# Stick-breaking attention with side work between its steps: other estimates for where the side work goes

## The chip, the cores and the metric

The kernel runs on one core of a Trainium2 chip. The metric is the device time of one execution in microseconds (us); less is better. Engines: TensorE (PE) for matmuls, VectorE (DVE), ScalarE (ACT), GpSimd (POOL), and SyncE (SP), which issues most DMA transfers.

## The reference, cut to what matters

One layer of a decoder trunk, 1024 positions of width 1024, in FP32. The part that the change touches is the mixer:

```
h = rms_norm(x, norm_mix_pre)
q, k, v, cb, cc, cx, g_att, g_conv = split(h @ w_in)
z = q.k / 8                              # 8 heads x 64, strictly causal
w[t,s] = sigmoid(z[t,s]) * prod_{s<j<t} (1 - sigmoid(z[t,j]))
y_att  = (w @ v) @ w_att_branch
y_conv = (cb * causal_dwconv3(cc * cx)) @ w_conv_branch
x = x + rms_norm((sigmoid(g_att)*y_att + sigmoid(g_conv)*y_conv) @ w_out, norm_mix_post)
```

A feed-forward block with a convolution follows (1024 to 2 x 2816, gelu, 2816 to 1024).

## The kernel before, in words

Every FP32 operand is split into a high and a low FP16 half, and a product is three matmuls (`PASSES`). So each weight tile of 512 KB needs work of its own before use: a load, a sum of squares (ACT, `square`), its total over partitions by a tiny matmul with ones (`total`), a power-of-two scale (three small DVE instructions, L89 to L92), the high half (ACT, L605) and the low half (DVE, L608).

**The attention loop.** There are 48 units, one for each pair of heads `j` (0 to 3), half of the queries `c`, and block `i` of 128 keys, taken from the last visible block down. `width` is the part of 512 queries that a unit touches (0.25 to 1). A turn `k` of the loop issues, in this order: `sums` of unit k (matmuls into the PSUM tile A, which exists once), `scores` of unit k+2 (matmuls into z, which exists once), a first stretch of fill, then `carry` and `sp_high` of k+1, `expa` of k, `sp_low` of k+1, `expz` of k+2, `times` of k, `bound` of k+2, `w_high_` of k, a second stretch of fill, then `softplus` of k+2, `w_low_` of k, `weigh` of k-1 (matmuls into o), and a third stretch of fill. The order on PE, DVE and ACT is exactly the one written (`manual_schedule`); each engine runs its own queue in order.

Two chains of waits cross the turns. `sums` of k+1 needs `carry`, `sp_high` and `sp_low` of k+1, and these need A of turn k; and `scores` of k+2 needs `expz` of k+1 to have read z.

**The fill.** Between those steps PE works on 400 chunks of three matmuls of 512 columns: the rest of v, the q, k, cb, cc, cx projections, the two gate projections (in the order of `FILL`), and last the tiles 4 to 7 of the convolution branch (`branch_fill`, output rows named ywc). Eight chunks fill one PSUM bank, and three banks are there for it (`bank`). A plan made before the loop says how many chunks each turn gets: `est[k]` is the estimated length of turn k, `att_pe[k]` the attention's own PE time in it, `lam` the factor that makes the total come out at 400 chunks of 0.65 us, and n = (est[k] * lam - att_pe[k]) / 0.65. The first stretch runs to 0.35 n, the second to 0.65 n, the third to n (`run_to`).

**The side work.** What the fill needs of ACT and DVE (evictions of banks, weight conversions, taps of the convolution, conversions of its result p to FP16 halves, L711 and L715) waits in lists of tasks in the class `Side`. At three points of each turn `point` adds `free[k]` to a credit of ACT and one of DVE, no higher than `CAP`, and lets tasks go ahead in order, evictions' list first. A step is issued while its engine's credit is above 0, or above a lower threshold where the task holds a bank or is urgent (`soon`); its cost is then taken off. What has not been done when a bank, a weight or (at branch tile 4, `q.drain`) the converted p is needed is forced: issued on the spot, whatever the credit. A weight's `total` borrows the bank of an eviction just done, and that bank is free only when the scale has been computed from it.

After the loop the gates go through a sigmoid, and the rest of the mixer and the feed-forward block follow; there the order of instructions is laid out by a scheduler and not written by hand.

Of the kernel before, what the change touches and what calls it, by code (L numbers as in the profile page):

```python
# [20 lines left out]
AF = mybir.ActivationFunctionType  # L21
ALU = mybir.AluOpType
# [6 lines left out]
NH = 512  # L29
# [1 line left out]
NFF = FF // P  # L31
EPS = 1e-6
EMAX = 1.2e19
FILL = ("q0 k0 q1 k1 cc0 cx0 q2 k2 cb0 cc1 cx1 cb1 cc2 cx2 q3 k3 cb2 cc3 cx3 cb3 gc0 ga0").split()
GROUPS = (2, 4, 4, 4, 4, 4)
KH = KD // 2
PASSES = ((0, 0), (0, 1), (1, 0))
# [2 lines left out]
class Layer:  # L40
# [235 lines left out]
    def mixer(self, mid):  # L276
        tc, nc, a = self.tc, self.nc, self.a
        hT = self.hp.tile([P, 2, KD, T], F16, tag="hT", name="hT")
        with ExitStack() as ph1:
# [368 lines left out]
            cv, dep, tail, last = {}, {}, [], [None]  # L648
# [92 lines left out]
            def branch(bi, d, pm, later=None):  # L741

                which = ("wc", "wa")[bi]
                w, inv = self.wdone[f"{which}{d // 2}"] if later else self.prep(f"{which}{d // 2}")
                outs = []
                sc = sgn[:, 4 * bi + d // 2:4 * bi + d // 2 + 1]
                if d % 2 == 0:
                    self.mul(sc, inv_x[bi], inv)
                y = self.xp.tile([P, T], F32, tag="x", name=f"y{which}{d}") if (bi, d) in ((0, 0), (0, 1)) else \
                    self.slot([P, T], F32, f"y{which}{d}")  # L750
                for c in range(2):
                    ps = bank(f"py{which}{d}_{c}") if later else pm.tile([P, NH], F32, tag="pm", name=f"py{which}{d}_{c}")
                    n = 0
                    for k in range(4):
                        for wi, hi in PASSES:
                            nc.tensor.matmul(ps, w[0][:, wi, ds((d % 2) * NH + k * P, P)],  # L756
                                             acts[bi][k][:, hi, ds(c * NH, NH)], start=n == 0, stop=n == 11)
                            n += 1
                        yield
                    if later:  # L760
                        def out(ps=ps, c=c):
                            last[0] = nc.vector.tensor_scalar(y[:, ds(c * NH, NH)], ps, sc, None, ALU.mult)
                        outs.append(Op("V", 0.7, out, f"py{which}{d}_{c}"))
                        later(outs[c:])
                    elif pm is self.pz:
                        nc.scalar.activation(y[:, ds(c * NH, NH)], ps, AF.Copy, scale=sc)
                    else:
                        nc.vector.tensor_scalar(y[:, ds(c * NH, NH)], ps, sc, None, ALU.mult)
                if later:
                    tail.append(lambda: self.sumsq(y, smy[:, 8 * bi + d:8 * bi + d + 1], f"y{which}{d}"))  # L770
                else:
                    self.sumsq(y, smy[:, 8 * bi + d:8 * bi + d + 1], f"y{which}{d}")
                ys[which, d] = y
# [3 lines left out]
            nu = len(units)  # L777
# [99 lines left out]
            def width(k):  # L877
                return (NH - units[k]["off"]) / NH if 0 <= k < nu else 0.0
# [19 lines left out]

            total, chunk = 400, 0.65
            att_pe = [2.6 * (width(k) * 0.33 + width(k + 2) * 0.33 + width(k - 1) * 0.33) for k in range(nu + 1)]  # L900
            est = [2.6 + 1.05 * (2 * width(k) + width(k + 1) + 2 * width(k + 2)) for k in range(nu + 1)]
            est[nu - 1] += 2.0
            est[nu] += 4.0
            att_v = [2.4 * (width(k) + width(k + 1) + 0.3 * width(k + 2)) * 0.9 for k in range(nu + 1)]
            lam = (sum(att_pe) + (total - 18) * chunk) / sum(est)
            free = [(est[k] * lam - att_v[k]) / 3 + 0.3 * (k > 36) for k in range(nu + 1)]
            fill = fills()
            state = dict(now=0.0)

            def run_to(t):  # L910
                while q.done < total and q.done < t:
                    if next(fill, "end") == "end":
                        q.done = total
                        return
                    q.done += 1
                    pump()

            with tc.manual_schedule(engines={ET.PE, ET.DVE, ET.Activation}):
                pump()
                run_to(6)  # L920
                at(scores, 0)
                at(expz, 0)
                at(bound, 0)
                q.point()
                run_to(10)
                at(softplus, 0)
                q.point()
                at(scores, 1)
                at(sp_high, 0)
                at(sp_low, 0)  # L930
                at(expz, 1)
                at(bound, 1)
                run_to(14)
                q.point()
                at(softplus, 1)
                run_to(18)
                q.point()
                base = 18.0
                for k in range(nu + 1):
                    n = (est[k] * lam - att_pe[k]) / chunk  # L940
                    at(sums, k)
                    at(scores, k + 2)
                    run_to(base + 0.35 * n)
                    at(carry, k + 1)
                    at(sp_high, k + 1)
                    at(expa, k)
                    if ready:
                        ready.pop(0)[1]()
                    q.point(free[k])
                    at(sp_low, k + 1)  # L950
                    at(expz, k + 2)
                    at(times, k)
                    at(bound, k + 2)
                    at(w_high_, k)
                    q.point(free[k])
                    run_to(base + 0.65 * n)
                    at(softplus, k + 2)
                    at(w_low_, k)
                    at(weigh, k - 1)
                    q.point(free[k])  # L960
                    run_to(base + n)
                    if ready:
                        ready[0][0]()
                    base += n
                run_to(total)
                for _ in fill:
                    pass
                for f in ready.pop(0) if ready else ():
                    f()
                q.drain("end")  # L970
                for name, t in wtasks.items():
                    if any(o.eng == "sum" for o in t.ops):
                        for o in t.ops[:2]:
                            if o.cost == 1.2:
                                o.f()
                        st = next(o.st for o in t.ops if o.st)
                        self.wraw[name] = st["sm"], [st["t"]]
                    else:
                        q.force(t, name)
                for which in ("gc", "ga"):  # L980
                    nc.scalar.activation(sig[which, 0], sig[which, 0], AF.Sigmoid)
# [423 lines left out]
class Side:  # L1405


    CAP = 1.3

    def __init__(self, pm, ones, nc):  # L1410
        self.pm, self.ones, self.nc = pm, ones, nc
# [47 lines left out]
    def advance(self, t, force=False):  # L1459
        while t.ops:  # L1460
            op = t.ops[0]
            if op.eng == "sum":
                if force:
                    host = getattr(t, "host", None)
                    if host is None:
                        if t in self.waiting:
                            self.waiting.remove(t)
                        ps = self.tile(f"pr_{len(self.late)}")
                        self.total(ps, op.st["rb"])
                        t.ops.pop(0).f(ps)  # L1470
                    while host and t.ops and t.ops[0] is op:
                        self.step(host)
                    continue
                if t not in self.waiting and not hasattr(t, "host"):
                    self.waiting.insert(0 if op.cost < 0 else len(self.waiting), t)
                return
            if not force:
                if t.t >= self.clock or not all(o.done for o in op.needs):
                    return
                if op.eng and self.credit[op.eng] <= (-1.5 if any(o.soon for o in t.ops) else 0):  # L1480
                    return
            if op.eng:
                self.credit[op.eng] -= op.cost
            self.step(t)
            if not op.eng or not t.ops or t.ops[0].eng != op.eng:
                t.t = self.clock
# [23 lines left out]
class Pair:  # L1510
# [3 lines left out]
    A = {1: (0, 0), 2: (0, 1), 3: (3, 0), 4: (1, 1), 5: (2, 0), 6: (2, 1), 7: (1, 0)}  # L1514
# [55 lines left out]
class Gates(Pair):  # L1570


    def out(self, name):
        return self.l.xp.tile([P, T], F32, tag="x", name=name)
# [93 lines left out]
```

## Time and profile before

| | us |
|---|---|
| median of 3 runs (lowest to highest) | 1352.25 (1351.61 to 1354.85) |
| the profiled execution | 1350.92 |
| its span, first to last instruction | 1349.2 |
| PE busy | 1311.9 |
| DVE busy | 1050.8 |
| ACT busy | 859.1 |

The mean granted TensorE clock of the profiled execution was 0.998 of full speed. The attention loop lies between about 69 and 425 us of the span: its 192 matmuls into A are 48 turns of four, the first at 69.0 us. Busy times are unions of the instructions' times on an engine. In rows of a group, the figures after the bar are the busy time in us, the mean length of one instruction in ns, then the engine's idle time just before them and what ended it. In rows of waits they are the total in us, the number and the longest.

### The profile page before, as it was taken

The numbers are of one execution on the slowest core, as the hardware profiler recorded it, in microseconds if no ns is written. First come the engines' busy times: TensorE is split into PE (matmuls) and PEld (weight loads), VectorE is DVE, ScalarE is ACT, GpSimd is POOL, SyncE is SP. The second block draws the span as 40 slices with busy tenths as digits, with TensorE's granted clock in tenths as the row PEclk, the third lists the DMA queues.
The fourth block names the chain that finished last, engine by engine and source line by source line (L and its number), as shares of the span: only waits on it lengthen the run. The fifth ranks groups of instructions, "written<-read, shape, count | busy, mean of one in ns | idle before, by whom it ended". The sixth has DMA issues, their size and how long they took to land. (4 is left out here: it accounts for less than half of the span.)

```text
span 1349.2 us, 16783 instructions
## 1 busy us (share of the span) xinstructions
PE 1311.9 (97%) x6491; PEld 590.0 (44%) x6491; DVE 1050.8 (78%) x1697; ACT 859.1 (64%) x1205; POOL 34.5 (3%) x58
## 2 busy tenths in 40 slices
PE   5999999999998999999999999999999999999997
PEld 3544444344433444444444444444444444444443
DVE  6568887878878957878788977975894896699855
ACT  6578877877777966665555676743752762576524
POOL 2000000000000000000110000000000000000002
PEclk9999999999999999999999999999999999999999
DMA  7011201101001222241431123222220312313126
GB/s 267 33 33 32 63 32 32 36 28 48 32 16 32 63 63 66 76 177 57 137 114 44 51 63 126 63 63 94 63 94 1 125 63 63 125 34 123 63 48 109
DMA packets 26608, 96.12 MB, mean 71 GB/s; under 512 B 3088, under 2 KB 3216, under 8 KB 26528
## 3 DMA queue, kind: packets, MB, share of 16 engines
q1 hardware_dynamic: 25088, 89.80, 20.2%
q0 software_dynamic: 1440, 5.24, 2.1%
q8 instruction: 51, 0.84, 0.3%
q14 instruction: 29, 0.24, 0.1%
HBM read 86.61 MB, written 8.42 MB: 70 GB/s over the span
## 5 line engine op out<-in xcount | busy, mean ns | idle before, releaser
L1538 PEld LDWEIGHTS <-wh_u 128*128 128x128 f16 x1848 | 178.8, 98 | 217.6 <-issue 3.8
L1312 PE MATMUL pd<-wdh,f 128*128 128x512 f16 (+1 forms) x1068 | 230.2, 377 | 2.7 <-ACT wdh L97 1.1
L1312 PEld LDWEIGHTS <-f 128*128 128x128 f16 x1068 | 104.5, 98 | 126.9 <-issue 4.0
L97 ACT ACTIVATE wh_u<-ws_u,sc 128x1024 f16<-128x1024 f32 (+1 forms) x66 | 64.7, 999 | 103.6 <-DVE sc L80 80.0
L1319 DVE SCALAR_TENSOR_TENSOR yacc<-pd,sd,yacc 128x512 f32<-128x512 f32 (+1 forms) x81 | 58.6, 742 | 73.4 <-PE pd L1312 65.9
L1538 PEld LDWEIGHTS <-wh_g 128*128 128x128 f16 x588 | 56.9, 98 | 68.7 <-issue 0.4
L1123 PE MATMUL py<-wh_wo,m 128*128 128x512 f16 x384 | 83.9, 379 | 0.0
L98 DVE SCALAR_TENSOR_TENSOR wh_u<-ws_u,sc,wh_u 128x1024 f16<-128x1024 f32 (+1 forms) x66 | 72.4, 1103 | 9.5 <-ACT wh_u L97 9.4
L824 ACT ACTIVATE sh<-sp 128x1024 f16<-128x1024 f32 (+3 forms) x48 | 40.4, 841 | 53.4 <-DVE sp L819 53.1
L1615 DVE SCALAR_TENSOR_TENSOR ugu<-cgu,cw_g,ugu 128x1023 f32<-128x1023 f32 (+1 forms) x44 | 56.4, 1283 | 11.3 <-ACT ugu L1613 10.9
L828 DVE TENSOR_TENSOR sh<-sp,sh 128x1024 f16<-128x1024 f32 (+3 forms) x48 | 45.9, 956 | 18.0 <-ACT sh L824 17.8
L1615 DVE SCALAR_TENSOR_TENSOR ua<-cau,cw_a,ua 128x1023 f32<-128x1023 f32 (+1 forms) x44 | 56.3, 1280 | 1.4 <-ACT ua L1613 1.3
L1123 PEld LDWEIGHTS <-m 128*128 128x128 f16 x384 | 37.5, 98 | 44.1
L819 DVE TENSOR_TENSOR sp<-A,sp 1x1024 f32<-1x1024 f32 (+3 forms) x40 | 35.9, 897 | 25.4 <-PE A L781 21.7
L850 ACT ACTIVATE w<-e 128x1024 f16<-128x1024 f32 (+3 forms) x48 | 40.5, 843 | 21.3 <-DVE e L845 20.4
L854 DVE SCALAR_TENSOR_TENSOR w<-e,w 128x1024 f16<-128x1024 f32 (+3 forms) x48 | 45.8, 954 | 9.2 <-ACT w L850 9.2
L814 ACT ACTIVATE sp<-e,one 128x1024 f32<-128x1024 f32 (+3 forms) x48 | 44.4, 925 | 6.0 <-DVE e L809 3.1
L845 DVE TENSOR_TENSOR e<-e,g 128x1024 f32<-128x1024 f32 (+3 forms) x48 | 45.7, 953 | 1.9 <-ACT g L841 1.8
L58 ACT ACTIVATE jk_u<-ws_u 128x1024 bf16<-128x1024 f32 x44 | 46.4, 1054 | 0.8
L756 PE MATMUL pywc<-p,wh_wc 128*128 128x512 f16 x192 | 43.2, 379 | 3.5 <-ACT sga L730 1.1
L211 PE MATMUL pcb<-hT,wh_cb 128*128 128x512 f16 x192 | 44.9, 379 | 0.9 <-DVE sc_cb L89 0.8
L800 ACT ACTIVATE e<-z,cz 128x1024 f32<-128x1024 f32 (+3 forms) x48 | 43.0, 897 | 3.6 <-PE z L781 3.6
(697 smaller groups left out, 2623.3 us busy)
## 6 DMA issues: line engine op xcount, KB each, us to landing
ws_u<-w_up_nt SPq DMA_DIRECT2D x44, 512.0 KB
ds<-w_down SPq DMA_DIRECT2D x22, 512.0 KB
wd<-w_down SPq DMA_DIRECT2D x22, 512.0 KB
ws_g<-w_in_nt SPq DMA_DIRECT2D x14, 512.0 KB
x<-x SPq DMA_DIRECT2D x8, 512.0 KB
ws_wo<-w_out SPq DMA_DIRECT2D x8, 512.0 KB
xr<-x SPq DMA_DIRECT2D x8, 512.0 KB
out<-x SPq DMA_DIRECT2D x7, 512.0 KB
```

Of the source, the lines that this page charges most:

```text
L58: self.nc.scalar.activation(self.junk(f"jk_{name}"), src, AF.Square, accum_out=acc)
L97: self.nc.scalar.activation(dst[:, 0, :], src, AF.Copy, scale=s)
L98: self.nc.vector.scalar_tensor_tensor(dst[:, 1, :], src, s, dst[:, 0, :], ALU.mult, ALU.subtract)
L211: nc.tensor.matmul(ps, w[:, wi, ds(k * P, P)], hT[:, hi, k, ds(c * NH, NH)], start=n == 0, stop=n == last)
L828: nc.vector.tensor_tensor(sh[:, 1, :, off:], u["sp"][:, :, off:], sh[:, 0, :, off:], ALU.subtract)
L845: nc.vector.tensor_tensor(e[:, :, off:], e[:, :, off:], u["g"][:, :, off:], ALU.mult)
L854: nc.vector.scalar_tensor_tensor(w[:, 1, :, off:], u["e"][:, :, off:], 2.0 ** 14, w[:, 0, :, off:], ALU.mult, ALU.subtract)
L1123: nc.tensor.matmul(ps, m16[k][:, hi, ds(tt * P, P)], wo[k][:, wi, sl], start=k == 0 and p == 0, stop=k == 7 and p == 2)
L1312: nc.tensor.matmul(pd[nh], f16[g][k][:, hi, ds(tt * P, P)], w[k][:, wi, ds(*part)], start=run is runs[0] and n == 0, stop=run is runs[-1] ...
L1319: nc.vector.scalar_tensor_tensor(y[:, sl], ps, sm[:, 0:1], y[:, sl], ALU.mult, ALU.add)
L1538: nc.tensor.matmul(ps, w[wt][:, wi, ds(wc * NH + k * P, P)], self.block(i, hi, k), start=first and n == 0, stop=n == 3 * KH - 1, skip_grou ...
L1615: nc.vector.scalar_tensor_tensor(u[:, lag:], c[:, :T - lag], sm[:, 2 - lag:3 - lag], u[:, lag:], ALU.mult, ALU.add)
```

## The change

- The estimate of a turn weighs `width(k)` and `width(k + 2)` by 1.9 instead of 2; 0.5 is added for turn 43 (`nu - 5`, with nu = 48), 2 for turn 44, 1 for turn 46 and 1 for turn 22. What was added for turns 47 and 48 stays.
- The estimate of DVE's own time in a turn is multiplied by 0.95 instead of 0.9, and `free` gets 0.4 instead of 0.3 added after turn 36.
- The second stretch of fill ends at 0.6 n instead of 0.65 n.
- The credit is held at 0.8 instead of 1.3, and an urgent step is issued while the credit is above -0.5 instead of -1.5.
- The two gate projections change places in the fill and in the order of weight loads.
- The two evictions of convolution branch tile 5 go to ACT (a copy with a scale) instead of DVE.

```diff
--- before.py
+++ after.py
@@ -31,7 +31,7 @@
 NFF = FF // P
 EPS = 1e-6
 EMAX = 1.2e19
-FILL = ("q0 k0 q1 k1 cc0 cx0 q2 k2 cb0 cc1 cx1 cb1 cc2 cx2 q3 k3 cb2 cc3 cx3 cb3 gc0 ga0").split()
+FILL = ("q0 k0 q1 k1 cc0 cx0 q2 k2 cb0 cc1 cx1 cb1 cc2 cx2 q3 k3 cb2 cc3 cx3 cb3 ga0 gc0").split()
 GROUPS = (2, 4, 4, 4, 4, 4)
 KH = KD // 2
 PASSES = ((0, 0), (0, 1), (1, 0))
@@ -758,9 +758,12 @@
                             n += 1
                         yield
                     if later:
-                        def out(ps=ps, c=c):
-                            last[0] = nc.vector.tensor_scalar(y[:, ds(c * NH, NH)], ps, sc, None, ALU.mult)
-                        outs.append(Op("V", 0.7, out, f"py{which}{d}_{c}"))
+                        by_v = "VAVV"[d - 4] == "V"
+
+                        def out(ps=ps, c=c, by_v=by_v):
+                            last[0] = nc.vector.tensor_scalar(y[:, ds(c * NH, NH)], ps, sc, None, ALU.mult) if by_v \
+                                else nc.scalar.activation(y[:, ds(c * NH, NH)], ps, AF.Copy, scale=sc)
+                        outs.append(Op("V" if by_v else "A", 0.7, out, f"py{which}{d}_{c}"))
                         later(outs[c:])
                     elif pm is self.pz:
                         nc.scalar.activation(y[:, ds(c * NH, NH)], ps, AF.Copy, scale=sc)
@@ -898,12 +901,16 @@
 
             total, chunk = 400, 0.65
             att_pe = [2.6 * (width(k) * 0.33 + width(k + 2) * 0.33 + width(k - 1) * 0.33) for k in range(nu + 1)]
-            est = [2.6 + 1.05 * (2 * width(k) + width(k + 1) + 2 * width(k + 2)) for k in range(nu + 1)]
+            est = [2.6 + 1.05 * (1.9 * width(k) + 1.0 * width(k + 1) + 1.9 * width(k + 2)) for k in range(nu + 1)]
+            est[nu - 5] += 0.5
+            est[nu - 4] += 2
+            est[nu - 2] += 1
             est[nu - 1] += 2.0
-            est[nu] += 4.0
-            att_v = [2.4 * (width(k) + width(k + 1) + 0.3 * width(k + 2)) * 0.9 for k in range(nu + 1)]
+            est[nu - 0] += 4.0
+            est[22] += 1
+            att_v = [2.4 * (width(k) + width(k + 1) + 0.3 * width(k + 2)) * 0.95 for k in range(nu + 1)]
             lam = (sum(att_pe) + (total - 18) * chunk) / sum(est)
-            free = [(est[k] * lam - att_v[k]) / 3 + 0.3 * (k > 36) for k in range(nu + 1)]
+            free = [(est[k] * lam - att_v[k]) / 3 + 0.4 * (k > 36) for k in range(nu + 1)]
             fill = fills()
             state = dict(now=0.0)
 
@@ -953,7 +960,7 @@
                     at(bound, k + 2)
                     at(w_high_, k)
                     q.point(free[k])
-                    run_to(base + 0.65 * n)
+                    run_to(base + 0.6 * n)
                     at(softplus, k + 2)
                     at(w_low_, k)
                     at(weigh, k - 1)
@@ -1405,7 +1412,7 @@
 class Side:
 
 
-    CAP = 1.3
+    CAP = 0.8
 
     def __init__(self, pm, ones, nc):
         self.pm, self.ones, self.nc = pm, ones, nc
@@ -1477,7 +1484,7 @@
             if not force:
                 if t.t >= self.clock or not all(o.done for o in op.needs):
                     return
-                if op.eng and self.credit[op.eng] <= (-1.5 if any(o.soon for o in t.ops) else 0):
+                if op.eng and self.credit[op.eng] <= (-0.5 if any(o.soon for o in t.ops) else 0):
                     return
             if op.eng:
                 self.credit[op.eng] -= op.cost
```

## The prediction

> **What bounds the kernel now.** I read the page first, then the busy time by stretch, then TensorE's waits, then the timeline around the longest of them. The page:
>
> ```profile
> span 1349.2 us, 16783 instructions
> PE 1311.9 (97%) x6491; PEld 590.0 (44%) x6491; DVE 1050.8 (78%) x1697; ACT 859.1 (64%) x1205; POOL 34.5 (3%) x58
> ```
>
> TensorE (PE) is busy in all but 37.3 us of the span, and the change adds and removes no matmul. Whatever it does must show as PE idle time. Busy time by stretch (length, then PE, weight load, DVE, ACT, POOL, granted clock, DMA share, GB/s) shows where that idle time lies:
>
> ```profile
> 0.00:69.00 69.00, 55.22 (x277) 28.93 (x278) 39.84 (x79) 39.35 (x58) 9.91 (x24) 1.00 0.42 147
> 69.00:236.00 167.00, 167.00 (x937) 69.70 (x936) 134.37 (x235) 129.38 (x172) 0.00 (x0) 1.00 0.13 39
> 236.00:262.00 26.00, 23.36 (x135) 9.69 (x132) 20.52 (x38) 20.02 (x32) 0.00 (x0) 1.00 0.13 41
> 300.00:313.00 13.00, 12.10 (x65) 4.87 (x64) 11.13 (x20) 10.84 (x13) 0.00 (x0) 1.00 0.13 42
> 391.00:427.00 36.00, 29.45 (x144) 11.69 (x141) 29.00 (x43) 23.45 (x30) 0.00 (x0) 1.00 0.10 30
> 427.00:640.00 213.00, 212.97 (x999) 96.58 (x1000) 169.69 (x262) 150.29 (x218) 1.30 (x2) 1.00 0.24 80
> 640.00:1349.20 709.20, 695.85 (x3290) 320.00 (x3288) 555.29 (x870) 395.39 (x568) 23.29 (x32) 1.00 0.26 79
> ```
>
> Length less PE time: 13.78 us before the attention loop, 0 in its first 167 us, 2.64 us at 236 to 262, 0.90 at 300 to 313, 6.55 at 391 to 427, and 13.38 after it. These seven sum to 37.25 us, so the stretches not shown have none. The edits reach only the loop: 10.1 us of idle time are all that they can win back. Who ended those waits:
>
> ```profile
> PE A L781 <- ACT g L841: 3.0, 1, 3.0
> PE pcc L1438 <- ACT u L664: 1.4, 1, 1.4
> PE pywc L756 <- ACT sga L730: 1.1, 1, 1.1
> PE pywc L756 <- DVE ywc L762: 0.8, 1, 0.8
> PE pcb L211 <- DVE sc_cb L89: 0.8, 1, 0.8
> PE pywc L756 <- DVE sc_wc L89: 0.8, 1, 0.8
> PE pywc L756 <- DVE p L715: 0.7, 1, 0.7
> PE z L781 <- ACT e L800: 0.5, 1, 0.5
> PE pcb L1438 <- DVE pf L667: 0.5, 1, 0.5
> ```
>
> Two kinds. In one PE waits for the chain of the attention turn itself (A, z). In the other (pcc, pcb, pywc) fill matmuls wait for a PSUM bank that ACT or DVE has yet to empty, or for an operand that DVE has yet to write. Neither engine is full in those stretches (DVE 29.00 of 36.00 us): they are late, by work put in front of what PE needs. The timeline of the tail (start, length, engine; turns 44 to 47 begin at the rows A at 382.64, 391.09, 401.70 and 411.20):
>
> ```profile
> 382.64 1.03 PE L781 MATMUL A<-sh,tri 128*128 128x512 f16 x4
> ...
> 386.89 3.21 ACT L711 ACTIVATE p<-pf,sp 128x1024 f16<-128x1024 f32 x3
> ...
> 390.01 1.10 ACT L800 ACTIVATE e<-z,cz 128x1024 f32<-128x1024 f32 x1
> ...
> 391.09 1.03 PE L781 MATMUL A<-sh,tri 128*128 128x512 f16 x4
> ...
> 391.75 3.67 DVE L715 SCALAR_TENSOR_TENSOR p<-pf,sp,p 128x1024 f16<-128x1024 f32 x3
> ...
> 396.47 1.28 DVE L715 SCALAR_TENSOR_TENSOR p<-pf,sp,p 128x1024 f16<-128x1024 f32 x1
> ...
> 398.17 1.22 DVE L819 TENSOR_TENSOR sp<-A,sp 1x1024 f32<-1x1024 f32 x1
> ...
> 401.70 1.03 PE L781 MATMUL A<-sh,tri 128*128 128x512 f16 x4
> ...
> 405.79 1.28 DVE L608 SCALAR_TENSOR_TENSOR wh_wc<-ws_wc,sc_wc,wh_wc 128x1024 f16<-128x1024 f32 x1
> ...
> 407.11 1.22 DVE L819 TENSOR_TENSOR sp<-A,sp 1x1024 f32<-1x1024 f32 x1
> ...
> 411.20 1.16 PE L781 MATMUL A<-sh,tri 128*128 128x512 f16 x4 [3.04 <-ACT g L841]
> ```
>
> Three conversions of side data in one burst on ACT (3.21 us) hold up the exponential at 390.01. Then four on DVE (3.67 and 1.28 us) stand before the carry (L819), which comes at 398.17, 6.0 us after the sums at 391.09 that it reads were done. A turn later a weight conversion (1.28 us) does the same, and PE stands still for 3.04 us. The middle has the same shape, two sums of squares in a row before the exponential that PE's scores wait for:
>
> ```profile
> 239.11 0.39 PE L781 MATMUL A<-sh,tri 128*128 128x128 f16 x4
> ...
> 250.86 1.05 ACT L58 ACTIVATE jk_p<-pf 128x1024 bf16<-128x1024 f32 x1
> ...
> 252.03 1.06 ACT L58 ACTIVATE jk_cb<-ws_cb 128x1024 bf16<-128x1024 f32 x1
> ...
> 253.09 1.09 ACT L800 ACTIVATE e<-z,cz 128x1024 f32<-128x1024 f32 x1
> ```
>
> The row A at 239.11 opens turn 24, so this is turns 24 to 26.
>
> **The change part by part.** The prices:
>
> ```profile
> 814.32 2.59 PE pu4c L1538 x12
> ...
> L211 PE MATMUL pga<-hT,wh_ga 128*128 128x512 f16 x48 | 11.2, 380 | 0.0
> ...
> L762 DVE TENSOR_SCALAR ywc<-pywc,sgn 128x512 f32<-128x512 f32 x8 | 5.8, 746 | 0.1
> ...
> L766 ACT ACTIVATE ywc<-pywc,sgn 128x512 f32<-128x512 f32 x8 | 5.3, 677 | 0.6 <-PE pr L76 0.3 <-PE pywc L756 0.2
> ```
>
> Twelve fill matmuls in 2.59 us are 0.216 us each, and a chunk of three 0.65 us. A matmul is drawn 0.380 us long though the next can start after 0.216, so an idle time of x in the profile costs x + 0.16.
>
> *The estimates.* `est` times `lam`, less the attention's own PE time (`att_pe`), divided by 0.65, is a turn's number of chunks. A full turn had (2.6 + 1.05 x 5) x 1.062 = 8.33 us, less 2.57, so 8.86 chunks. Now it has (2.6 + 1.05 x 4.8) x 1.072 = 8.19 us, so 8.64. Turn 44, with 2 added, goes to 11.93; turn 43 from 9.19 to 9.79, turn 46 from 6.75 to 8.32, turn 22 from 7.28 to 8.81. Turns 47 and 48 stay within 0.1. The running sum at the start of turn 43 goes from 348.6 to 343.5. So 5.1 chunks, 3.3 us of matmuls, are taken from turns 0 to 42, at 0.1 to 0.2 chunk a turn, and laid on turns 43, 44 and 46.
>
> *Tail, now 6.55 us idle.* Turns 43 and 44 get 0.60 + 3.07 = 3.67 chunks, 2.4 us more of PE work while ACT and DVE do the p conversions. That covers the 1.1 and 0.7 us waits of turn 45 and leaves 0.5 us. The 3.04 us wait of turn 46 has three things against it: that 0.5, turn 46's own 1.57 chunks (1.0 us), and one of the two evictions that branch tile 5 moves from DVE to ACT (0.75 us; I count one of two, since the other may end behind the carry). About 0.8 stays, and the two waits after it (0.8 and 0.8, one for a weight's scale, one for the last tile's eviction, which stays on DVE) stay too. 6.55 becomes about 2.4: **-4.1 us**, with ends at 0 (the waits only move) and -6.55.
>
> On ACT the two evictions take 2 x 0.68 us in a stretch where it has 36.00 - 23.45 = 12.5 us free; without that cover they would cost 1.4 us. The trace has ACT at 677 ns and DVE at 746 for this same form, so the move is no loss for the tile itself. The Trainium skill, "ScalarE: Activation LUTs", Rules for kernel authors, speaks against it: multiplications belong on VectorE, up to three times faster there per element in bf16. By that factor two evictions would be 4.5 us on ACT, an estimate, still inside the free 12.5; the rows of this FP32 form from PSUM say otherwise, and they decide.
>
> *Middle, now 2.64 us idle.* Turn 22's 1.53 chunks are 1.0 us more of cover just ahead of turns 24 to 26. With `CAP` 0.8 instead of 1.3 a sum of squares (cost 1.2) leaves the credit at -0.4, not 0.1, so the second waits for a later point: 1.2 us less before the exponential. The exponential's wait is only one of four, so I count a further 0.4: **-1.4 us**, ends 0 and -2.64.
>
> *Hidden part.* Four waits gone at 0.16: **-0.6 us**, ends 0 and -1.8 (eleven waits).
>
> *Smaller credit.* The threshold for work that holds a bank goes from -1.5 to -0.5. A heavy DVE step now stops an eviction behind it at the same point (0.8 - 1.3 = -0.5, blocked), so evictions come a point later at times. An eviction not done when `bank` wants the fourth bank is forced, and PE waits for it at its queue's head. Behind that wait stand the chunk, then the next weigh, sums and scores. Such a wait costs 0.5, 0.8 or 1.4 us (the pf, sc_cb and u rows). The profile shows no count of near misses. I take one more, **+0.9 us**, the middle of these rows. Ends: -0.9 (the 0.90 us at 300 goes) and +5 (five or six more).
>
> *Thinner cover elsewhere.* 0.1 us less per turn. The 167 us without any idle say that most turns have room; only turns like those around 300 to 313 pay: **+0.3 us**, ends 0 and +3.3 (all that was taken).
>
> *At nothing:* the two gate projections change places. Their 512 KB loads, sum, conversion and 16 chunks are of equal size, so SP's queue only carries the other name first, and the sga wait will read sgc. The second fill point at 0.6 instead of 0.65 puts half a chunk (0.3 us) behind the weigh. `att_v` and `free` change a point's share by about 0.1, within what the cap cuts off. Cover for these is the backlog of fill in front of PE; without it they would cost at most those 0.3 us. The stages after the loop shift with its end; their order may be laid out differently, 0 with ends at -1 and +1.
>
> Sum: -1.4 - 4.1 - 0.6 + 0.9 + 0.3 = -4.9 us. The profiled execution took 1350.92 us (its span and 1.72 around it), 1.33 under the median of the runs, so 1346.0 for its like, and 1352.25 - 4.9 = **1347.4 us** for the median.
>
> **The rivals.** *The p conversions are forced.* With one DVE conversion per point (credit -0.5 after each) two of the four may be left when branch tile 4 begins in turn 45, where `drain` puts them in front of the carry: 2 x 1.28 = 2.6 us come back. Against it: turn 44 is 2 us longer, which is more points' worth of ACT and DVE time before the drain. Result -4.9 + 2.6 = -2.3, 1350.0 us.
>
> *Evictions late everywhere (slower).* The smaller credit is felt in all 48 turns, the added cover in four. There are 400 / 8 = 50 fill halves. If ten evictions more come forced, at 0.8 + 0.16, it is -4.9 - 0.9 + 9.6 = +3.8, and with one more +4.8: 1357.0 us. From six on the gain is gone. For it: six of the nine waits above (pcc, sga, ywc, sc_cb, sc_wc, pf) are of that kind already. Against it: 80% or less of DVE and ACT is used, and the 0 idle of the first 167 us.
>
> *The clock.* If the tail's waits join into one that outlasts 3.0 us, the longest that the trace shows at clock 1.00, TensorE may be slowed: 16 matmuls at twice 0.216 would add 3.5 us, and with no tail gain it is -4.9 + 4.1 + 3.5 = +2.7, 1355.0 us. The Trainium skill, "TensorE: Matmul & The Clock Gate", Part 1, says so: an idle window of about 3.4 us halves the clock. The granted clock of 1.00 agrees so far.
>
> **How the numbers follow.** A measurement of this kernel tells about 0.3%, 4.1 us, from no change. Forecast 0.56, conversions forced 0.21, evictions late 0.20, clock 0.03. The forecast's own range is 1343 to 1350 with about four fifths of it beyond -4.1: faster 0.45. The rest of it, the first rival and the clock are within: 0.35. Slower 0.20. The range needs the forecast's best end (two thirds of the loop's idle time and its hidden part won, about -9.5: 1342.7) and must reach to where the slower rival begins: 1342.5 to 1356.5.
>
> **What would show it.** Right: PE idle in the last 36 us of the loop near 2.4 us, that around turns 24 to 26 near 1.2, no wait of A for g over 1 us; bursts of at most two p conversions on ACT; two evictions of ywc on ACT inside the loop. Wrong: waits of fill matmuls for evictions or scales (L89, L664, L667, L730) in more than seven places, or any PE idle in the first 160 us; p conversions directly ahead of the carry in turn 45; a clock below 1.00; or a gain that comes from behind the loop.

## The result, and the profile after

The changed kernel took 1340.2 us (median of 5 runs, 1340.12 to 1340.71) against 1351.69 us before (median of 5, 1350.65 to 1354.85). The ratio is 0.9914 with a 95% interval of 0.9902 to 0.9925: faster by 0.86%, 11.5 us. The forecast was 1347.4 with a range of 1342.5 to 1356.5. The sign was right, the gain more than twice the forecast's 4.9 us, and the time lies 2.3 us below the range. The page of the changed kernel:

```profile
span 1338.4 us, 16787 instructions
PE 1310.8 (98%) x6491; PEld 589.7 (44%) x6491; DVE 1049.7 (78%) x1695; ACT 859.2 (64%) x1207; POOL 34.4 (3%) x58
```

PE is busy for 1.1 us less than before (1311.9), and the span is 10.8 us shorter: nine tenths of what went is idle time. Busy time by stretch, in the columns of the prediction; the tail now lies at 376 to 417:

```profile
69.00:236.00 167.00, 167.00 (x940) 69.49 (x937) 136.34 (x239) 131.35 (x176) 0.00 (x0) 1.00 0.12 37
236.00:262.00 26.00, 26.00 (x155) 11.13 (x154) 21.38 (x40) 21.20 (x33) 0.00 (x0) 1.00 0.15 50
300.00:313.00 13.00, 13.00 (x73) 5.14 (x71) 11.55 (x23) 10.09 (x12) 0.00 (x0) 1.00 0.13 42
376.00:417.00 41.00, 39.91 (x201) 16.34 (x200) 32.08 (x49) 30.56 (x37) 0.00 (x0) 1.00 0.09 26
417.00:631.00 214.00, 214.00 (x1005) 97.08 (x1004) 171.75 (x267) 151.63 (x220) 1.30 (x2) 1.00 0.25 82
631.00:1338.40 707.40, 694.69 (x3284) 319.37 (x3282) 554.43 (x866) 395.51 (x566) 23.23 (x32) 1.00 0.26 79
```

The loop's idle time is 1.09 us instead of 10.1. All of the middle's is gone, and of nine listed waits one is left, the one for the last eviction:

```profile
PE pywc L756 <- DVE ywc L764: 0.9, 1, 0.9
```

9.0 us of shown idle time, with 0.16 hidden in each of about nine waits (1.4), make 10.4. Behind the loop, 13.38 less 12.71 are 0.7 more; this part is not the loop's, for e10 below has the same idle time in the loop and 13.3 behind it. Less the 0.2 us by which the first row A comes later (69.27 us against 69.03) that is 10.9; the span lost 10.8.

The timeline of the tail (turns 44 to 47 begin at 376.02 and at the rows A):

```profile
382.85 2.17 ACT L711 ACTIVATE p<-pf,sp 128x1024 f16<-128x1024 f32 x2
...
384.12 2.47 DVE L715 SCALAR_TENSOR_TENSOR p<-pf,sp,p 128x1024 f16<-128x1024 f32 x2
384.93 1.13 ACT L817 ACTIVATE sp<-e,one 128x1024 f32<-128x1024 f32 x1
385.97 2.17 ACT L711 ACTIVATE p<-pf,sp 128x1024 f16<-128x1024 f32 x2
386.41 1.03 PE L784 MATMUL A<-sh,tri 128*128 128x512 f16 x4
387.14 2.48 DVE L715 SCALAR_TENSOR_TENSOR p<-pf,sp,p 128x1024 f16<-128x1024 f32 x2 [0.54 <-ACT p L711]
...
390.33 1.22 DVE L822 TENSOR_TENSOR sp<-A,sp 1x1024 f32<-1x1024 f32 x1
...
394.50 1.03 PE L784 MATMUL A<-sh,tri 128*128 128x512 f16 x4
...
402.06 1.03 PE L784 MATMUL A<-sh,tri 128*128 128x512 f16 x4
```

The p conversions come two and two, with the softplus (L817) of the turn between. On DVE all four still stand ahead of the carry at 390.33, two of them in turn 45, as the first rival said. But the carry (390.33) now begins 2.9 us after its sums were done (386.41 + 1.03), not 6.0, and PE has its work in that time: turn 44 lasts 10.39 us instead of 8.45.

### The profile page after: what moved, and what is told of

It is laid out like the page before. It is cut to its first block, busy times and chain, and to the rows that moved or that the text cites. A ratio compares the mean times of both kernels' runs of the same rounds, so it can differ in the third digit from the quotient of the medians.

```text
span 1338.4 us, 16787 instructions
## 1 busy us (share of the span) xinstructions
PE 1310.8 (98%) x6491; PEld 589.7 (44%) x6491; DVE 1049.7 (78%) x1695; ACT 859.2 (64%) x1207; POOL 34.4 (3%) x58
## 5 line engine op out<-in xcount | busy, mean ns | idle before, releaser
L1622 DVE SCALAR_TENSOR_TENSOR ugu<-cgu,cw_g,ugu 128x1023 f32<-128x1023 f32 (+1 forms) x44 | 56.2, 1277 | 11.3 <-ACT ugu L1620 10.9
L822 DVE TENSOR_TENSOR sp<-A,sp 1x1024 f32<-1x1024 f32 (+3 forms) x40 | 35.9, 897 | 30.0 <-PE A L784 25.6
L831 DVE TENSOR_TENSOR sh<-sp,sh 128x1024 f16<-128x1024 f32 (+3 forms) x48 | 45.8, 954 | 13.5 <-ACT sh L827 13.3
L817 ACT ACTIVATE sp<-e,one 128x1024 f32<-128x1024 f32 (+3 forms) x48 | 44.4, 924 | 4.0 <-DVE e L812 2.7
L211 PE MATMUL pcx<-hT,wh_cx 128*128 128x512 f16 x192 | 44.9, 379 | 0.0
```

The costliest lines, as they stand in the source:

```text
L211: nc.tensor.matmul(ps, w[:, wi, ds(k * P, P)], hT[:, hi, k, ds(c * NH, NH)], start=n == 0, stop=n == last)
L831: nc.vector.tensor_tensor(sh[:, 1, :, off:], u["sp"][:, :, off:], sh[:, 0, :, off:], ALU.subtract)
L1622: nc.vector.scalar_tensor_tensor(u[:, lag:], c[:, :T - lag], sm[:, 2 - lag:3 - lag], u[:, lag:], ALU.mult, ALU.add)
```

## The experiments

Twelve kernels, each compared with the kernel before on the same chip. "Middle" and "tail" are PE's idle time in 69 to 360 us and 360 to 430 us of the profiled execution (length less PE time in the view by stretch).

| kernel | median, us | lowest | ratio to before (95%) | middle | tail |
|---|---|---|---|---|---|
| before | 1350.8 to 1351.9 | 1350.05 | 1 | 3.54 | 6.59 |
| changed | 1340.2 | 1340.12 | 0.9914 (0.9902-0.9925) | 0.00 | 1.09 |
| e1 old credit | 1344.89 | 1343.67 | 0.9958 (0.9943-0.9973) | 2.06 | 2.16 |
| e2 no end turns | 1350.58 | 1349.7 | 0.9996 (0.9987-1.0005) | 1.21 | 6.58 |
| e3 no turn 22 | 1345.87 | 1343.63 | 0.9960 (0.9946-0.9974) | 2.00 | 1.70 |
| e4 estimates alone | 1344.86 | 1343.93 | 0.9957 (0.9942-0.9972) | 1.85 | 2.75 |
| e5 credit alone | 1347.76 | 1346.96 | 0.9975 (0.9965-0.9984) | 1.11 | 5.15 |
| e6 branch tile on DVE | 1341.62 | 1340.34 | 0.9926 (0.9912-0.9941) | 0.00 | 1.08 |
| e7 end turns alone | 1347.27 | 1346.14 | 0.9968 (0.9954-0.9982) | 3.93 | 2.56 |
| e8 last tile on ACT | 1340.9 | 1340.5 | 0.9921 (0.9906-0.9936) | 0.00 | 1.22 |
| e9 end turns and credit | 1342.79 | 1342.71 | 0.9932 (0.9916-0.9949) | 0.55 | 1.82 |
| e10 estimates and credit | 1341.43 | 1340.1 | 0.9922 (0.9906-0.9938) | 0.00 | 1.08 |
| e11 old cap | 1344.07 | 1343.71 | 0.9945 (0.9930-0.9959) | 2.07 | 2.32 |
| e12 old threshold | 1341.39 | 1340.36 | 0.9923 (0.9907-0.9938) | 0.00 | 0.95 |

Runs of one kernel differ by up to 5 us, in part by what the TensorE clock did in them, which is told under e12. A median of a few runs carries that too, so the idle times carry the comparison.

**Undoing one part.** e1:

```diff
-    CAP = 0.8
+    CAP = 1.3
-  if op.eng and self.credit[op.eng] <= (-0.5 if any(...) else 0):
+  if op.eng and self.credit[op.eng] <= (-1.5 if any(...) else 0):
```

> The changed kernel with the credit as before (cap 1.3, threshold -1.5). Theory 1 (cover): the estimates alone removed the waits, because the idle time sat just behind the turns that got more chunks; then this stays within 2 us of the changed kernel's 1340.2, with no idle at 391 to 427 but for the last eviction's 0.9. Theory 2 (bursts): the smaller credit removed them by spreading the side work; then two thirds or more of the 11.5 us come back (1348 or more), with waits of PE for evictions and for the exponential at several places. Theory 3 (near misses): no edit has a place of its own, each loses part: 1342 to 1347.

4.7 us lost by the medians, 3.1 by the idle time, which is back in both places, 2.06 and 2.16. Neither of the first two theories' numbers: theory 3's range.

e2:

```diff
-            est[nu - 5] += 0.5
-            est[nu - 4] += 2
-            est[nu - 2] += 1
```

> The changed kernel without the 0.5, 2 and 1 for turns 43, 44 and 46. Theory 1: the tail's idle time comes back, 4 to 7 us, and nothing in the middle: 1344 to 1347, PE idle in turns 45 to 47 near 5. Theory 2: the bursts stay gone, so at most 2 us come back: below 1342. Theory 3: 1342 to 1347 with idle also at places far from the tail.

More than any theory said: no measurable gain is left in the time. In idle time 2.3 us of it are left: the middle has 1.21 instead of 3.54. The two longest groups of this kernel's waits, and the stretches around the longest (all columns as above, granted clock before the last two):

```profile
PE pywc L756 <- DVE ywc L764: 5.2, 2, 2.8
PE pywc L756 <- ACT sgc L730: 1.1, 1, 1.1
```

```profile
421.60:424.90 3.30, 0.47 (x4) 0.02 (x2) 1.58 (x4) 3.06 (x5) 0.00 (x0) 1.00 0.00 0
...
425.40:428.30 2.90, 2.90 (x8) 1.06 (x7) 2.83 (x3) 1.36 (x2) 0.00 (x0) 0.50 0.00 0
428.30:440.00 11.70, 11.70 (x58) 5.32 (x57) 10.10 (x20) 8.67 (x11) 0.00 (x0) 0.99 0.01 1
```

The tail's idle time is as before, 6.58 us, though other instructions end its waits, and PE then ran at half clock: 8 matmuls in 2.9 us. At the granted 0.50 half of those 2.9 us, some 1.5, went there though they count as busy. The loop also began 0.9 us later in this run (first row A at 69.90 us against 69.03 before), so the two together hide what the idle time won.

e3:

```diff
-            est[22] += 1
```

> The changed kernel without the 1 for turn 22. Theory 1: 1 to 3 us come back, as PE waits in turns 24 to 26, and the tail stays free: 1341 to 1343. Theory 2: nothing comes back, within 1 us of 1340.2. Theory 3: 1341 to 1345, with waits also outside turns 24 to 26.

```profile
PE A L784 <- ACT g L844: 1.0, 2, 0.5
PE pywc L756 <- DVE ywc L764: 0.8, 1, 0.8
PE pywc L756 <- DVE sc_wc L89: 0.8, 1, 0.8
PE z L784 <- ACT e L803: 0.5, 2, 0.3
PE pk L211 <- DVE sc_cx L89: 0.3, 1, 0.3
PE pcc L1444 <- ACT u L664: 0.2, 1, 0.2
```

Only the last row (0.2 us) lies in turns 24 to 27. The waits for g and e lie at 307 to 330 us, and the sc_wc wait in the tail. Turn 22's chunk and a half shifts the fill after it against the turns, and its absence is felt far from turn 22.

**One part alone.** e4:

```diff
-            est = [2.6 + 1.05 * (2 * width(k) + width(k + 1) + 2 * width(k + 2)) ...]
+            est = [2.6 + 1.05 * (1.9 * width(k) + 1.0 * width(k + 1) + 1.9 * width(k + 2)) ...]
+            est[nu - 5] += 0.5
+            est[nu - 4] += 2
+            est[nu - 2] += 1
+            est[22] += 1
```

> The kernel before with the new est lines alone (weights 1.9, turns 22, 43, 44, 46); credit, shares, second fill point, gates and branch tile as before. Theory 1: three quarters or more of the gain, 1340 to 1343. Theory 2: a third or less, 1348 or more. Theory 3: between them, 1343 to 1348.

Three fifths of the idle time that the whole change wins (5.5 of 9.0 us), with idle times close to e1's: theory 3's range again. One wait is new: 0.4 us at 170 us, in the stretch that had none before; e1 and e11, which share the new estimates and the old cap, have it too.

e5:

```diff
-    CAP = 1.3
+    CAP = 0.8
-  ... <= (-1.5 if any(...) else 0)
+  ... <= (-0.5 if any(...) else 0)
```

> The kernel before with the smaller credit alone (cap 0.8, threshold -0.5). The runs so far: without the end turns' additions 10.4 us of the gain are gone, with the old credit 4.7. Theory 1 (cover first): the tail keeps its waits, and the credit wins at most what the middle has, 2.6 + 0.9 us: 1347 to 1351. Theory 2 (bursts): it wins about the 4.7 that its removal cost, tail included: 1346 to 1348. The prediction's slower rival (evictions late) says 1352 or more, with more waits of fill matmuls for evictions and scales than the six of before.

```profile
PE A L781 <- ACT g L841: 3.2, 1, 3.2
PE pywc L756 <- ACT sga L730: 1.1, 1, 1.1
PE pywc L756 <- DVE ywc L762: 0.8, 1, 0.8
PE pcb L211 <- DVE sc_cb L89: 0.8, 1, 0.8
PE pcb L211 <- DVE sc_cx L89: 0.3, 1, 0.3
```

3.0 us won by the medians, 3.9 by the idle time. The middle's waits around turns 24 to 26 (2.64 us) are gone, and of the kinds that the slower rival feared there are fewer, not more. The tail keeps its two large ones. 1347.76 lies in theory 1's range and in theory 2's; that the tail keeps 5.15 of its 6.59 us speaks for theory 1 there. The profiled run, 1351.03 us, is the longest of ten, with two stretches at half clock.

e7:

```diff
+            est[nu - 5] += 0.5
+            est[nu - 4] += 2
+            est[nu - 2] += 1
```

> The kernel before with the additions for turns 43, 44 and 46 alone. Theory 1: the tail's waits go without help of the credit, 4 to 6 us: 1345.5 to 1347.5, middle as before (2.6 + 0.9 us idle). Theory 2: bursts remain in the tail, under 3 us: 1348.5 or more. Theory 3 (near misses): anything between 1343 and 1351, with waits at other places of the middle than before, since every turn's share of chunks moves.

3.5 us won by the medians, 3.6 by the idle time: the tail falls from 6.59 to 2.56, and the middle grows from 3.54 to 3.93. Theory 1's number, near the forecast's -4.1 for the tail. But the middle's waits have moved, as theory 3 said: none is left at 300 to 313 us, and 1.1 us are new at 330.

**Putting them together.** e9 is e7 and e5 in one kernel.

> The kernel before with two edits, the additions for turns 43, 44 and 46 and the smaller credit. Each alone won 3.5 and 3.0 us, all edits together 10.5 to 11.5. If the two are the whole mechanism (cover in the tail, no bursts elsewhere) and act together: 1340 to 1342.5. If they only add up, 1343.5 to 1345, with waits left in turns 24 to 27 or 32 to 34. If other edits carry the rest (turn 22, weights 1.9), waits at just those turns and 1343 or more.

2.4 us of idle time are left of 10.1, so 7.8 are won. Alone the two won 3.9 (e5) and 3.6 (e7), 7.5 in sum: in idle time they add up, and neither needs the other. The medians' 3.0, 3.5 and then 9.1 us would say that they help each other, but they hold what the clock did as well. The median is above the first range partly because the profiled run, 1342.71 us, holds a stretch at half clock behind the loop like e12's below. What is left in the middle, 0.55 us, lies in turns 25 and 26, just behind turn 22, whose addition e9 lacks.

e10 is e4 and e5 in one kernel, so the change without its four small edits.

> The kernel before with all of the new est lines and the smaller credit, so the changed kernel without the new shares (0.95, 0.4), the second fill point at 0.6, the gates' exchange and the branch tile on ACT. If these four are side matters: 1340 to 1341.5, one wait left. If they matter, 1342 or more, with waits for ywc in turns 46 to 48 (branch tile) or for the weigh's o (second point).

The loop's idle time is the changed kernel's (0.00 and 1.08) with the same single wait, and its lowest run, 1340.1, too. The new shares, the second fill point, the gates' exchange and the branch tile on ACT are together worth nothing that shows. And the credit is worth about the same whatever stands beside it: 3.9 us of idle time alone (before to e5), 4.1 on the end turns (e7 to e9), 3.5 on all estimates (e4 to e10), 3.1 in the changed kernel (e1).

**Which half of the credit.** e11 puts back the cap, e12 the threshold:

```diff
-    CAP = 0.8
+    CAP = 1.3
```

> The changed kernel with the cap at 1.3 again and the threshold at -0.5. Both back cost 4.7 us. If the burst that a saved-up credit allows is the harm (cap): 1343 to 1346. If it is the debt that bank-holding steps may run up (threshold): within 1 us of 1340.2.

```diff
-  ... <= (-0.5 if any(...) else 0)
+  ... <= (-1.5 if any(...) else 0)
```

> The changed kernel with the threshold at -1.5 again and the cap at 0.8. The mirror of the run with the old cap: if the cap is what counts, within 1 us of 1340.2; if the threshold is, 1343 to 1346, with PE waiting for evictions that ACT and DVE have behind chain steps.

It is the cap: idle 2.07 and 2.32 with the old one, 0.00 and 0.95 with the old threshold. The timeline of e11 around 250 us, then that of the changed kernel:

```profile
250.06 1.04 ACT L58 ACTIVATE jk_p<-pf 128x1024 bf16<-128x1024 f32 x1
...
251.22 1.06 ACT L58 ACTIVATE jk_cb<-ws_cb 128x1024 bf16<-128x1024 f32 x1
...
252.28 1.13 ACT L817 ACTIVATE sp<-e,one 128x1024 f32<-128x1024 f32 x1
...
253.44 0.95 DVE L822 TENSOR_TENSOR sp<-A,sp 1x768 f32<-1x768 f32 x1 [0.89 <-ACT sp L817]
...
256.08 0.68 ACT L664 ACTIVATE u<-pcc,cv 128x512 f32<-128x512 f32 x1
...
256.81 0.16 PE L1445 MATMUL pcc<-rb_k,ones 128*128 128x1 bf16 x1 [1.24 <-ACT u L664]
```

```profile
248.92 1.04 ACT L58 ACTIVATE jk_p<-pf 128x1024 bf16<-128x1024 f32 x1
...
249.96 1.13 ACT L817 ACTIVATE sp<-e,one 128x1024 f32<-128x1024 f32 x1
...
251.56 0.95 DVE L822 TENSOR_TENSOR sp<-A,sp 1x768 f32<-1x768 f32 x1 [1.49 <-PE A L784]
...
254.20 0.68 ACT L664 ACTIVATE u<-pcc,cv 128x512 f32<-128x512 f32 x1
...
256.62 1.04 ACT L58 ACTIVATE jk_cb<-ws_cb 128x1024 bf16<-128x1024 f32 x1
```

With 1.3 two sums of squares run back to back before the softplus, the carry (L822) waits for that softplus, and the eviction u, 2.6 us behind the carry, makes PE wait 1.24 us. With 0.8 the second one comes a turn later, the carry waits only for its sums A, and behind u, again 2.6 us after the carry, PE does not wait.

That the cap breaks up such pairs holds for the whole loop. Counted in each trace, from the first sums of the loop to the last: stretches between two steps of the chain in which ACT runs 2.0 us or more of side work (steps that are not the attention's own). The five kernels with cap 1.3 (before, e1, e4, e7, e11) have 14 or 15 of them, the nine with 0.8 have 2 to 4. The wait shown is 1.24 of the 3.3 us that the old cap brings back; the others were not traced to their pairs.

e12's profiled run took 1342.93 us, its lowest 1340.36, and only the first has a trace. e10's profiled run took 1340.1, with the same PE idle time as e12's (28.1 and 28.0 us over the span), so the 2.8 us between these two are time in which PE counts as busy. One stretch, in e12 and then in e10:

```profile
705.00:711.90 6.90, 4.91 (x27) 2.60 (x26) 6.03 (x11) 4.59 (x9) 0.00 (x0) 1.00 0.00 1
711.90:715.40 3.50, 3.50 (x10) 1.27 (x9) 3.50 (x7) 2.67 (x5) 0.00 (x0) 0.51 0.00 0
```

```profile
705.00:711.90 6.90, 4.91 (x26) 2.56 (x25) 6.04 (x12) 4.82 (x9) 0.00 (x0) 1.00 0.00 0
711.90:715.40 3.50, 3.50 (x18) 1.61 (x17) 2.87 (x5) 2.16 (x4) 0.00 (x0) 1.00 0.00 0
```

Behind the same 2 us of idle time, far from the loop, one run had 3.5 us at half clock (10 matmuls where the other has 18, 1.7 us lost) and the other not. The rest comes from the start of the program, again e12 first:

```profile
20.00:24.00 4.00, 4.00 (x14) 1.56 (x13) 3.56 (x4) 3.02 (x5) 2.48 (x2) 1.00 0.78 228
```

```profile
20.00:24.00 4.00, 4.00 (x20) 1.79 (x19) 3.56 (x4) 3.00 (x5) 2.50 (x2) 1.00 0.75 228
```

In both runs the first matmuls of 512 columns follow each other at 0.427 us and later ones at 0.216. e12 changes over at 22.5 us, e10 at 20.1 (no record of the granted clock exists before that, so its column says 1.00), and e12's loop begins at 69.9 us instead of 68.7, 1.2 us later.

**The branch tiles.** e6 and e8:

```diff
-                        by_v = "VAVV"[d - 4] == "V"
+                        by_v = "VVVV"[d - 4] == "V"
```

> The changed kernel with branch tile 5's two evictions back on DVE. If the move to ACT was part of what freed the tail (1.5 us off DVE), 0.8 to 2 us come back as waits for ywc evictions or for the carry's chain in turns 46 to 48: 1341 to 1342.5. If the added chunks cover DVE anyway, it stays within 0.6 us of 1340.2.

Idle time as in the changed kernel (0.00, 1.08), lowest run 1340.34: the cover hides DVE's two evictions. The median, 1.4 us higher, comes from two of four runs that took 2.4 to 2.9 us more than the others; the profiled one is of the shorter kind.

```diff
-                        by_v = "VAVV"[d - 4] == "V"
+                        by_v = "VAVA"[d - 4] == "V"
```

> The changed kernel with branch tile 7's two evictions on ACT as well. The only wait over 0.2 us left in the loop is PE's 0.95 us for tile 7's last eviction on DVE, which stands there behind the low half of o and a weight's scale. ACT is idle for 1.0 us just then. If the place in DVE's queue is the cause: 0.3 to 0.8 us faster, 1339.4 to 1339.9. If the bank is simply read too late after its last matmul (0.68 us on ACT as on DVE 0.74), no difference, within 0.3 us. If it delays the table load and the sigmoids behind it on ACT and these count: slower by up to 1.

The last wait is 0.8 us instead of 0.9, and a new one of 0.3 us follows behind the loop. The bank is needed right after its last matmul; whoever empties it, PE waits. No version found is faster than the changed kernel.

## Why the prediction was right or wrong, point by point

*Where the gain can come from:* right. It is PE's idle time in the loop, 10.1 us shown, and nothing else moved it by more than 0.7.

*The tail, -4.1:* right in mechanism, three quarters in size. The end turns' chunks alone won 4.0 of the tail's 6.6 (e7), but the whole change wins 5.5. Of the waits that I let stay, the two before the last eviction's went too. What the term leaves out is the credit, to which I gave nothing in the tail: alone it wins 1.4 us there (e5), and 1.7 on top of the new estimates (e4 to e10). It does not replace the cover: without the end turns all the rest leave the tail's 6.58 (e2).

*The middle, -1.4, and the 0.90 us at 300:* mis-sized. All 3.54 us went. I gave the cap 0.4 us; alone it frees turns 24 to 26 (e5). Turn 22, to which I gave the rest, is needed, but only in part where I put it: without it the waits come up at 307 to 330 us (e3), or, with the old weights of 2, in turns 25 and 26 (e9).

*Smaller credit, +0.9:* the step that failed, its sign. Less the 0.4 us that I gave the cap in the middle, the credit was to cost 0.5 us. It wins 3.1 to 4.1 us of idle time in each of the four pairs of kernels listed under e10. That is most of the 5.9 us by which the span's 10.8 passed the forecast's 4.9. The harm that I priced, an eviction blocked at 0.8 - 1.3 = -0.5, needs the new threshold; with the old one it may pass, and the idle time is the same (e12, 0.95 against 1.09), so it costs nothing that shows. What I left out is that the cap keeps heavy steps from holding up the chain, and so makes evictions come earlier, because they stand behind the chain in the same queue (u above). Old cap: 3.3 us of idle time more (e11). With it falls the slower rival. The estimates, by contrast, were forecast about right: turn 22, the tail and the thinner cover were to give -1.0 - 4.1 + 0.3 = -4.8, and they won 5.5 us of idle time alone (e4) and 5.2 on top of the credit (e5 to e10).

*Thinner cover, +0.3:* not seen; the first 167 us have no idle time as before, and neither has the rest. With an edit missing it does appear: at 307 to 330 us (e3) and, with the old cap, at 170 us (e1, e4, e11), so it is not nothing by itself.

*Hidden part, -0.6:* about -1.4, since nine waits went and not four.

*At nothing:* right for the gates, the second point and the shares, taken together (e10). The branch tile on ACT, to which I gave 0.75 us, is worth nothing (e6): cover hid the evictions. The first rival's premise came true, two p conversions before the carry, without its price. The clock rival did not come true here, but did in e2 and e5, and behind the loop in e5, e9 and e12.

*The range:* its lower end was worked out wrongly. Two thirds of the loop's 10.1 us and the hidden 1.8 are 7.9 us, not 9.5, which is four fifths. The best ends of the terms themselves, -2.64 - 6.55 - 1.8 - 0.9, make -11.9 and 1340.4 us, close to the 1340.2 measured. And DVE is not 80% busy or less everywhere: in 300 to 313 us it is 86% (11.13 of 13.00).

What stays open: why turn 22 and the weights of 1.9 are just enough, and why e2, which has them without the end turns, has more idle time (7.8 us) than the credit alone (6.3). e9 and e10 differ by these, and they take the last 0.55 in the middle and 0.7 in the tail. All chunks after turn 22 shift by them, and I found no single wait that explains it; theory 3, near misses that any shift can open or close, is what e3 and e7 fit best, but it is argued, not shown.

## What to carry to other kernels

Where one engine is full and others work just ahead of it, its few idle microseconds can come from pairs of heavy side steps in front of a chain step, as they did here. Two things helped, and each did without the other: a limit on how much side work one point may issue, and cover put where the chain is longest. When a term is priced from one harm that an edit may do, price also what the same edit takes out of the chain's way. Let the range reach as far as the best ends of its own terms.

Judge a change of a few microseconds, and whether two such changes add up, by the idle times of the stage, since medians also carry what the clock did: alone the two parts won 3.9 and 3.6 us of idle time and together 7.8, while the medians said 3.0, 3.5 and 9.1.

## What the runs showed of the hardware that was not expected

The clock can fall to half after less idle time than the 3.04 us that it survived in the kernel before. In e2 a wait of 2.8 us was enough, and in e12 about 2 us spread over 7. What decides in these traces is how the idle time lies. The granted clock in their records changes only at multiples of 3.41 us after the moment at which the matmuls first go over to 0.216 us apart (20.7 us into the span before, 20.5 in e5, 22.5 in both e2 and e12). Two such steps of the kernel before, two of e5, one of e12 and one of e2:

```profile
406.38:409.79 3.41, 1.77 (x9) 0.68 (x7) 2.65 (x3) 3.38 (x6) 0.00 (x0) 1.00 0.48 138
409.79:413.20 3.41, 2.00 (x9) 0.87 (x9) 2.61 (x6) 2.93 (x5) 0.00 (x0) 1.00 0.05 20
```

```profile
402.81:406.22 3.41, 1.31 (x7) 0.49 (x5) 2.13 (x3) 3.30 (x7) 0.00 (x0) 1.00 0.51 156
406.22:409.64 3.42, 2.34 (x6) 0.86 (x6) 2.36 (x2) 2.94 (x5) 0.00 (x0) 0.50 0.01 2
```

```profile
708.56:711.97 3.41, 1.42 (x9) 0.71 (x8) 3.17 (x5) 2.26 (x4) 0.00 (x0) 1.00 0.00 0
```

```profile
718.76:722.18 3.42, 1.53 (x7) 0.65 (x7) 3.28 (x6) 2.84 (x5) 0.00 (x0) 1.00 0.00 0
```

The wait of 3.04 us before lies across two steps, which have 1.6 and 1.4 us without PE work, and the clock stayed. e5's wait of 3.2 us puts 2.10 into one step, and the next is at half clock. e12's step has 1.99 and is followed by half clock (the row at 711.90 above), e2's last one has 1.89 and is not. Counted over all 14 traces: the clock fell after every step with 1.99 us or more (in e2 2.83, in e5 2.10 and 1.99, in e9 and e12 1.99, and near the end of each program 2.4 to 3.4), and after none with 1.89 or less. That the limit, between 1.89 and 1.99 us of a step, is the same in other kernels is not shown.

So the same 2 us of idle time behind the loop cost e5, e9 and e12 a step at half clock and the other eleven traces nothing. This fits the Trainium skill's "TensorE: Matmul & The Clock Gate", Part 1, that the window of about 3.4 us is free-running; its rule of thumb of no PE-idle gaps over about 3.4 us is not enough by these rows. A wait removed can be worth more than its length, here up to 1.7 us more per step.
